# Coefficient tables by direction, the last table block by halves, scan coefficients copied earlier, and early output halves of two blocks kept in SBUF

## The chip, the cores and the metric

The kernel runs on one core of a Trainium2 chip. The metric is the device time of one execution, in microseconds (us). A core has five engines with instruction queues of their own, each in order: TensorE (PE in the profile; PEld is its weight load), VectorE (DVE), ScalarE (ACT), GpSimd (POOL) and SyncE (SP), which here issues DMAs. An instruction starts when its engine has done all that stand ahead of it in the queue and when the semaphores that it waits for are set. A wait therefore also holds whatever stands behind the waiting instruction on that engine.

## The reference

The program is a bidirectional encoder of four layers: an S5 state-space mixer, a gated MLP with a centred convolution, a differential attention layer and a second such MLP, for 512 positions of 1024 channels. The change lies in the S5 mixer alone:

```
u = h.reshape(bsz, seq, 64 groups, 16 channels)
for direction in range(2):
    abar = exp(step * lam)                     # complex, per group and state (64 states)
    bbar = (abar - 1) / lam * b                # complex
    bu   = einsum('blgc,gpc->lbgp', u, bbar)
    s    = associative_scan(abar, bu, reverse=(direction == 1))
    y   += einsum('lbgp,gcp->blgc', s_re, c_re) - einsum('lbgp,gcp->blgc', s_im, c_im)
g = gelu(y);  out = g * sigmoid(g @ glu_w + glu_b)
```

The other three layers are matrix products with norms, a softmax and gates between them.

## The kernel before

One function, `trunk`, holds the whole program. The mixer is worked in chunks of 8 positions: 64 chunks, whose states are chained by a scan of 64 steps, and inside a chunk by a small Toeplitz product.

First come the powers of the coefficients. PRh and PIh hold the powers of abar, FRh and FIh those times the input factor (64 rows of each direction, 8 powers, 64 groups). `cmul` builds powers from powers on VectorE (6 operations); `tok` is the RMS norm's chain of small operations, and `chains` writes several such chains by turns. `ftab` (L369) copies FRh and FIh into a PSUM table F: tag "F", two buffers of one bank each. A table of before holds 16 groups of both directions and takes 8 copies of 64x128; two of the first table's are on VectorE, the others on ScalarE (L385).

Then the block loop (L528) runs over 16 blocks b = (p2, dr): 8 groups of one direction each. In a block VectorE does a product `vmul` (L502, with the first half of F), a product `vmul2` (L509, second half, into PSUM) and their sum (L539). The product of block b+1 is issued ahead of the sum of block b. Every odd block has `kfix` (L516, L518) between, which repairs the kernel block that ScalarE copied in the odd block before. TensorE transposes the sum in two halves (vtp, L547), ScalarE copies each out (vt, L549); between the halves TensorE does `in_mm` of the block before (ips, L476), which ScalarE copies into IZ (L483). After them come the kernel products (kps, L563), copied by ScalarE after odd blocks (kq, L573), and transposed and copied by `kt` (ktp L489; KF, KB L491). At a block's end ScalarE gets table copies: pieces of `ftab` after blocks 3, 4, 7 and 8, and pieces of `tables` (8 copies of PR and PI, L451, which GpSimd needs for the output weights W, and 12 of the scan coefficients sct, L459). GpSimd builds the chunks of W all the while (L431, L433, L436); for five later ones TensorE adds the two parts and ScalarE copies the sum (L441 to L443).

The scan (L661) is a chain on VectorE: two products (L678), two sums (L681, which read IZ) and two sums into the next state (L683) a step. After every 8 steps `states` (L648) writes the states into IZ with 8 copies of 64x256, on ScalarE but for the last four. The list EV says at which step something else is written among these: w is a chunk of W, i is `intra` (L617, the Toeplitz product of output block bk, 16 matmuls), f and b are `out_half` (L633, the state part of rows that are ready early, forward and backward), y is ScalarE's copy of an intra result into SBUF (ys, L657). Since ScalarE works in order, a y that stands ahead of a `states` group delays that group when its own input is late.

After the scan `out_fin` closes the eight output blocks. For 0 to 5 it adds the halves that were missing (L725: 32 matmuls of 32 rows), for 6 and 7, of which only the intra part is in ys, it makes all rows (L713: 32 matmuls of 64 rows), and VectorE adds ys (L732). A gelu (L734), transposes (L746) and casts with a residual split (L750, L751: `chan`) lead to the first matrix product (L778). From there TensorE works nearly without a break to the end of the program.

Of the kernel before, what the change touches and what calls it, by code (L numbers as in the profile page):

```python
# [9 lines left out]
F32 = mybir.dt.float32  # L10
# [27 lines left out]
def trunk(ctx, tc, xs, xt, sp, bx, cx, sv, vec, lamv, biasw, wglu, wup, wdn, wv, wqk, wo, out):  # L38
# [353 lines left out]
    chains(ftab(0))  # L392
    chains(ftab(1))
# [10 lines left out]
    fgen = iter([])  # L404

# [92 lines left out]
    def vmul(b):  # L498
        p2, dr = divmod(b, 2)
        fl = (p2 % 2) * 8  # L500
        vb = vs.tile([128, 8, 8, 16], F32, tag="vb", name="vb", bufs=4)
        V.tensor_tensor(vb, bc(Xb, dr * 64 + p2 * 8), kbc(F[p2 // 2][0][:, dr, :, fl:fl + 8]), op=ALU.mult)  # L502
        return vb

    def vmul2(b):
        p2, dr = divmod(b, 2)
        fl = (p2 % 2) * 8
        vb2 = ps1.tile([128, 8, 8, 16], F32, tag="vb2", name="vb2", bufs=1)
        V.tensor_tensor(vb2, bc(Yb, dr * 64 + p2 * 8), kbc(F[p2 // 2][1][:, dr, :, fl:fl + 8]), op=ALU.mult)  # L509
        return vb2  # L510
# [977 lines left out]
```

## Time and profile before

| | us |
|---|---|
| median of 3 runs | 1249.82 (1247.38 to 1250.08) |
| profiled execution | 1246.88 |
| its span in the trace | 1245.1 |
| busy: PE, DVE, ACT, POOL | 1175.8, 824.9, 581.6, 253.5 |
| block loop 21 to 84: DVE busy of 63.00 | 59.60 |
| scan 92 to 150: DVE busy of 58.00 | 57.82 |
| 200 to 1245: PE busy of 1045.00 | 1027.14 |

The profiled execution is one execution; 1.78 us of it lie around the span. A timeline row has the start, the duration (of all instructions where several are merged, with xcount), the engine, the line, the operation with its tiles (out<-in), and in brackets the idle time just before it and what ended this. The clock column is the clock granted to TensorE as a share of full speed.

### The profile page before, as it was taken

How to read it: one execution, taken by the hardware profiler on the slowest of the kernel's cores; microseconds unless marked ns; L12 is line 12 of the kernel's file. 1: busy time of each engine (PE TensorE's matmuls, PEld its weight loads, DVE VectorE, ACT ScalarE, POOL GpSimd, SP SyncE). 2: the span in 40 equal slices, each digit the busy share in tenths (PEclk: the TensorE clock that was granted, in tenths of full speed). 3: DMA queues.
4: the chain of work that ended last, by engine and by line, in shares of the span. 5: the costliest groups of instructions: out<-in, count | busy, mean ns of one | idle time of the engine just before them, and what ended most of it. 6: DMA issues, size and time to landing. Idle time of an engine off the chain costs nothing.

```text
span 1245.1 us, 16497 instructions
## 1 busy us (share of the span) xinstructions
PE 1175.8 (94%) x6338; PEld 930.0 (75%) x6338; DVE 824.9 (66%) x1650; ACT 581.6 (47%) x1001; POOL 253.5 (20%) x271
## 2 busy tenths in 40 slices
PE   3875899999999999999998999999999999999996
PEld 1663588888878888878876777678888878888786
DVE  7989866676752467754339899976767643566634
ACT  6864655444431244333337777755444422344431
POOL 3899434000000000011033444523000000000011
PEclk8997999999999999999999999999999999999998
DMA  5005322122233222132332323221222233122222
GB/s 219 2 2 136 135 75 102 68 102 84 75 117 115 68 102 101 58 106 77 99 123 82 90 74 87 88 73 67 98 71 99 81 117 125 68 92 78 93 94 68
DMA packets 23391, 112.32 MB, mean 90 GB/s; under 512 B 2704, under 2 KB 5392, under 8 KB 16144
## 3 DMA queue, kind: packets, MB, share of 16 engines
q1 hardware_dynamic: 21472, 108.64, 25.7%
q0 software_dynamic: 1280, 2.10, 0.9%
q8 instruction: 50, 0.82, 0.3%
q10 hardware_dynamic: 560, 0.52, 0.1%
q14 instruction: 29, 0.24, 0.1%
HBM read 102.86 MB, written 2.10 MB: 84 GB/s over the span
## 4 chain that ended last, share of the span: by engine, by line
PE 83%; DVE 14%; ACT 2%; issue 1%; DMA 0%; SPq 0%; DVEq 0%; ACTq 0%
PE ps L779 20%; PE ps L778 20%; PE ps L780 20%; DVE scn L678 2%; PE pj L778 2%; PE pj L780 2%; PE pj L779 2%; DVE St L683 1%; PE vps L1088 1%; DVE qkt L1141 1%; PE vps L1090 1%; PE vps L1089 1%; DVE acc L681 1%; PE po L779 1%; PE po L780 1%; PE po L778 1%
## 5 line engine op out<-in xcount | busy, mean ns | idle before, releaser
L778 PE MATMUL ps<-xhi,hi 128*128 128x512 f32 x672 | 266.9, 397 | 0.0
L779 PE MATMUL ps<-xlo,hi 128*128 128x512 f32 x672 | 265.7, 395 | 0.0
L780 PE MATMUL ps<-xhi,lo 128*128 128x512 f32 x672 | 264.1, 393 | 0.0
L139 ACT ACTIVATE hi<-raw 128x1024 fp32r<-128x1024 f32 (+2 forms) x216 | 184.1, 874 | 113.5 <-PE ps L779 85.8
L141 DVE TENSOR_TENSOR lo<-raw,hi 128x1024 fp32r<-128x1024 f32 (+3 forms) x178 | 188.3, 1077 | 43.5 <-ACT hi L139 41.8
L903 DVE TENSOR_TENSOR tpb<-ps,rb 128x512 f32<-128x512 f32 x88 | 60.8, 693 | 149.7 <-PE ps L780 144.5
L905 ACT ACTIVATE acc<-tpb,vect 128x512 f32<-128x512 f32 x88 | 71.6, 816 | 168.2 <-DVE tpb L903 168.2
L780 PEld LDWEIGHTS ps<-xhi,lo 128*128 128x128 f32 x672 | 126.1, 188 | 31.5
L778 PEld LDWEIGHTS ps<-xhi,hi 128*128 128x128 f32 x672 | 126.1, 188 | 30.6
L779 PEld LDWEIGHTS ps<-xlo,hi 128*128 128x128 f32 x672 | 126.2, 188 | 29.5
L779 PE MATMUL ps<-act,hi 128*128 128x512 f32 (+1 forms) x374 | 144.1, 385 | 0.2
L778 PE MATMUL ps<-act,hi 128*128 128x512 f32 (+1 forms) x374 | 142.8, 382 | 0.0
L780 PE MATMUL ps<-act,lo 128*128 128x512 f32 (+1 forms) x374 | 142.1, 380 | 0.0
L803 POOL COPY ssum<-sqt 128x512 f32<-128x512 f32 x4 | 2.5, 627 | 658.5 <-ACT sqt L800 658.5
L981 DVE TENSOR_TENSOR h<-ps,h 128x512 f32<-128x512 f32 x30 | 20.7, 690 | 107.5 <-PE ps L780 107.5
L141 POOL TENSOR_TENSOR lo<-raw,hi 128x512 fp32r<-128x512 f32 (+1 forms) x38 | 61.0, 1611 | 114.2 <-ACT hi L139 114.1
L778 PEld LDWEIGHTS ps<-act,hi 128*128 128x128 f32 x374 | 70.3, 188 | 15.8
L780 PEld LDWEIGHTS ps<-act,lo 128*128 128x128 f32 x374 | 70.2, 188 | 15.9 <-DVE lo L141 1.4
L779 PEld LDWEIGHTS ps<-act,hi 128*128 128x128 f32 x374 | 70.2, 188 | 15.3 <-DVE act L922 1.1
L911 DVE SCALAR_TENSOR_TENSOR acc<-tpb,vect,acc 128x512 f32<-128x512 f32 x88 | 66.2, 752 | 3.1
L910 DVE SCALAR_TENSOR_TENSOR acc<-tpb,vect,acc 128x512 f32<-128x512 f32 x88 | 65.5, 744 | 0.6 <-ACT acc L905 0.6
L921 ACT ACTIVATE act<-acc 128x512 fp32r<-128x512 f32 x44 | 27.9, 634 | 66.2 <-DVE acc L920 66.2
(260 smaller groups left out, 2035.7 us busy)
## 6 DMA issues: line engine op xcount, KB each, us to landing
raw<-wup SPq DMA_DIRECT2D x44, 1024.0 KB, 4.8
raw<-wdn SPq DMA_DIRECT2D x32, 704.0 KB, 4.0
raw<-wqk SPq DMA_DIRECT2D x16, 512.0 KB, 3.5
raw<-wglu SPq DMA_DIRECT2D x4, 1024.0 KB, 4.9
raw<-wv SPq DMA_DIRECT2D x8, 512.0 KB, 3.5
raw<-wo SPq DMA_DIRECT2D x4, 1024.0 KB, 4.8
bias<-biasw SPq DMA_DIRECT2D x8, 448.0 KB, 4.1
cxt<-cx SPq DMA_DIRECT2D x1, 2064.0 KB, 15.8
```

What stands on the lines that cost most here:

```text
L139: S.activation(hi[:, h0:h1], self.raw[i][:, h0:h1], AF.Copy)
L141: eng.tensor_tensor(lo[:, h0:h1], self.raw[i][:, h0:h1], hi[:, h0:h1].bitcast(F32), op=ALU.subtract)
L678: V.tensor_tensor(prd[dr], cur[:, dr].unsqueeze(1).to_broadcast([128, 2, 2, 32]), cft[dr], op=ALU.mult)
L778: PE.matmul(ps, lhsT=wh, rhs=xh, start=first, stop=False)
L779: PE.matmul(ps, lhsT=wh, rhs=xl, start=False, stop=False)
L780: PE.matmul(ps, lhsT=wl, rhs=xh, start=False, stop=last)
L903: V.tensor_tensor(tb[:, 1:513], ps, state["rb"], op=ALU.mult)
L905: S.activation(acc, tb[:, 1:513], AF.Identity, bias=cb, scale=cw[1])
L910: V.scalar_tensor_tensor(acc, tb[:, 0:512], cw[0], acc, op0=ALU.mult, op1=ALU.add)
L911: V.scalar_tensor_tensor(acc, tb[:, 2:514], cw[2], acc, op0=ALU.mult, op1=ALU.add)
L921: S.activation(hi, a0, AF.Copy)
L981: V.tensor_tensor(h[:, m], ps, h[:, m], op=ALU.add)
```

## The change

1. `ftab(dr, g8)` makes one table for one direction and 32 groups, in 4 copies of 64x256. Two are made at the start, `ftab(0, 0)` and `ftab(1, 0)`. The other two follow at the end of blocks 6 and 7, when the two buffers have been read for the last time. Blocks 0 to 7 read the first two, blocks 8 to 15 the others.
2. The powers 2 and 3 are made ahead of `tok`, those from 4 on by turns with it. The eight PR and PI copies stand after blocks 1 and 2, the sct copies from block 3 on.
3. In block 15 `kfix(6)` comes first, then product and sum by halves of 128x512. The last vtp takes the bank of vb2, and the last two ips have a bank each of tag "F".
4. The copies of the scan's coefficients (`scan_tables`) stand on ScalarE ahead of the last two IZ copies.
5. Output blocks 6 and 7 get intra and both early halves during the scan, late (steps 46 to 53), and are then copied to ys; after the scan `out_fin` makes only their missing halves, as for the others.
6. The last group of states is copied in two parts: 6 of 8 states at step 61, 2 at step 63.

```diff
-    chains(ch_f47(), tok())
+    chains(cmul(FRh[:, 2:4], FIh[:, 2:4], FRh[:, 0:2], FIh[:, 0:2], *pk(2, 2), 2))
+    chains(cmul(FRh[:, 4:8], FIh[:, 4:8], FRh[:, 0:4], FIh[:, 0:4], *pk(4, 4), 4), tok())
...
-    def ftab(g4):
-
-        f = ps1.tile([128, 4, 8, 16], F32, tag="F", name="F", bufs=2)
...
+    def ftab(dr, g8):
+
+        f = F[dr, g8] = ps1.tile([128, 2, 8, 32], F32, tag="F", name="F", bufs=2)
+        for ti, tab in enumerate((FRh, FIh)):
+            src = tab[64 * dr:64 * dr + 64, :, g8 * 32:g8 * 32 + 32]
+            if dr == 0:
+                src = src[:, ::-1]
+            for ri in range(2):
+                dst = f[64 * ri:64 * ri + 64, ti]
+                sg = 1.0 if ri + ti == 0 else -1.0
+                if g8 + dr == 0 and ti == 0:
+                    V.tensor_scalar(dst, src, sg, None, op0=ALU.mult)
+                else:
+                    S.mul(dst, src, sg)
...
-    chains(ftab(0))
-    chains(ftab(1))
+    ftab(0, 0)
+    ftab(1, 0)
...
-            if b == 14:
-                vtt["i"] = ps1.tile([128, 8, 2, 64], F32, tag="vb2", name="ips", bufs=1)
-            ips = vtt["i"][:, 4 * (b - 14):4 * (b - 13)]
+            ips = ps1.tile([128, 4, 2, 64], F32, tag="F", name="ips", bufs=2)
...
-    def vmul2(b):
+    def vmul2(b, vb):
...
+        if b < 15:
+            V.tensor_tensor(vb2, bc(Yb, dr * 64 + p2 * 8), tab, op=ALU.mult)
+            V_next(b)
+            V.tensor_tensor(vb, vb, vb2, op=ALU.add)
+        else:
+            kfix(6)
+
+            for q in range(2):
+                part = slice(4 * q, 4 * q + 4)
+                V.tensor_tensor(vb2[:, part], bc(Yb, dr * 64 + p2 * 8)[:, part], tab[:, part], op=ALU.mult)
+                V.tensor_tensor(vb[:, part], vb[:, part], vb2[:, part], op=ALU.add)
...
+    def V_next(b):
+        nonlocal vnext
+        if b % 2 == 1 and b > 1:
+            kfix(b // 2 - 1)
+        vnext = vmul(b + 1)
...
-                vtp = (ps1.tile([128, 4, 128], F32, tag="F", name="vtp", bufs=2) if last else
+                vtp = (ps1.tile([128, 8, 128], F32, tag="vb2", name="vtp", bufs=1)[:, 0:4] if last else
...
         if b == 15:
+            for _ in tgen:
+                pass
+            scan_tables()
             in_mm(14, vtt.pop(14))
             in_mm(15, vtt.pop(15))
...
-            if b in (3, 7):
-                fgen = ftab(2 + b // 7)
-            for _ in range(4):
-                next(fgen, None)
-            for _ in range((0, 3, 3, 0, 0, 2, 2, 0, 0, 2, 2, 2, 2, 2)[b] if b < 14 else 0):
+            if b in (6, 7):
+                ftab(b - 6, 1)
+            for _ in range((0, 4, 4, 2, 2, 2, 0, 0, 2, 2, 2, 2, 2, 2)[b] if b < 14 else 0):
...
-    EV = ((11, 'w', 8), (12, 'w', 9), (22, 'w', 10), (23, 'i', 7), (23, 'y', 7), (24, 'i', 6), (24, 'y', 6), (25, 'i', 0),
...
+          (38, 'b', 3), (39, 'w', 13), (43, 'w', 14), (44, 'w', 15), (46, 'i', 6), (46, 'f', 6), (47, 'b', 6), (47, 'y', 6),
+          (48, 'i', 4), (48, 'f', 4), (49, 'b', 4), (51, 'i', 7), (52, 'f', 7), (52, 'b', 7), (53, 'y', 7), (54, 'i', 5),
+          (54, 'f', 5), (55, 'b', 5))
...
+        if s == 61:
+            for dr in range(2):
+                states(St, 56, dr, 0, 6)
         if sl == 7:
             for dr in range(2):
-                states(St, s - 7, dr)
+                states(St, s - 7, dr, 6 if s == 63 else 0)
...
     def out_fin(bk):
-        if bk >= NB:
+        if bk in ASIDE:
             yb[bk] = ps2.tile([128, 4, 8, 16], F32, tag="yp", name="yp", bufs=6)
...
-                        PE.matmul(yb[bk][64 * e:64 * e + 64, pl], lhsT=IZ[:, :, dr, e, pr],
-                                  rhs=W[pr // 8][:, dr, (pr % 8) * 2 + e], start=(pl + dr == 0), stop=True,
-                                  skip_group_check=True)
...
+                    PE.matmul(yp[r0:r0 + 32, pl], lhsT=IZ[:, j0:j0 + 32, dr, e, pr],
+                              rhs=W[pr // 8][:, dr, (pr % 8) * 2 + e], start=bk in ASIDE and pl == 0, stop=True,
+                              skip_group_check=True, tile_position=(0, r0))
```

The order changes at three places. The first is on ScalarE and VectorE in blocks 6 and 7. On ScalarE before, from the vt of block 6's first half on (vt_695, ips_697 and vt_720 are of block 7; F_732 is a table that block 12 is the first to read):

```order
L549 COPY vt_636<-vtp_631 128x512
L483 COPY IZ_78<-ips_638 128x64x2x4
L549 COPY vt_661<-vtp_656 128x512
L459 ACTIVATE sct_71<-PRh_212 64x32
L459 ACTIVATE sct_71<-PIh_213 64x32
L549 COPY vt_695<-vtp_690 128x512
L483 COPY IZ_78<-ips_697 128x64x2x4
L549 COPY vt_720<-vtp_715 128x512
L573 COPY kq_730<-kps_663 128x512
L385 ACTIVATE F_732<-tsc_92 64x128 x4
```

ScalarE after, from the same place on (vt_689, ips_691 and vt_714 are of block 7; F_663 is the table of direction 0, F_726 of direction 1):

```order
L562 COPY vt_627<-vtp_622 128x512
L472 COPY IZ_78<-ips_629 128x64x2x4
L562 COPY vt_652<-vtp_647 128x512
L379 ACTIVATE F_663<-tsc_92 64x256 x4
L562 COPY vt_689<-vtp_684 128x512
L472 COPY IZ_78<-ips_691 128x64x2x4
L562 COPY vt_714<-vtp_709 128x512
L589 COPY kq_724<-kps_654 128x512
L379 ACTIVATE F_726<-tsc_92 64x256 x4
```

Two groups of four copies have come in, one ahead of block 7's vt, one behind kq_724. On VectorE before, from the second product of block 7 on (vb_687 and vb_746 are the products of blocks 8 and 9, F_496 was written in blocks 3 and 4):

```order
L509 TENSOR_TENSOR vb2_682<-bxt_93,F_277 128x1024
L516 SCALAR_TENSOR_TENSOR kq_606<-svt_72,kps_545 128x16 x2
L518 TENSOR_TENSOR kq_606<-kq_606,kps_545 128x2x16
L502 TENSOR_TENSOR vb_687<-bxt_93,F_496 128x1024
L539 TENSOR_TENSOR vb_628<-vb_628,vb2_682 128x1024
L509 TENSOR_TENSOR vb2_744<-bxt_93,F_496 128x1024
L502 TENSOR_TENSOR vb_746<-bxt_93,F_496 128x1024
L539 TENSOR_TENSOR vb_687<-vb_687,vb2_744 128x1024
```

VectorE after (vb_681 and vb_740 are the products of blocks 8 and 9, vb_619 the sum of block 7):

```order
L500 TENSOR_TENSOR vb2_676<-bxt_93,F_273 128x1024
L515 SCALAR_TENSOR_TENSOR kq_597<-svt_72,kps_538 128x16 x2
L517 TENSOR_TENSOR kq_597<-kq_597,kps_538 128x2x16
L491 TENSOR_TENSOR vb_681<-bxt_93,F_663 128x1024
L502 TENSOR_TENSOR vb_619<-vb_619,vb2_676 128x1024
L500 TENSOR_TENSOR vb2_738<-bxt_93,F_663 128x1024
L491 TENSOR_TENSOR vb_740<-bxt_93,F_726 128x1024
L502 TENSOR_TENSOR vb_681<-vb_681,vb2_738 128x1024
```

The sequence is the same, but the product of block 8 reads F_663 and stands ahead of the sum of block 7, and that of block 9 reads F_726 and stands ahead of the sum of block 8.

The second place is on ScalarE at the end of the block loop. Before (scn0 and scn1 are the scan's coefficients of the two directions):

```order
L483 COPY IZ_78<-ips_1096 128x64x2x4
L549 COPY vt_1119<-vtp_1114 128x512
L549 COPY vt_1141<-vtp_1136 128x512
L483 COPY IZ_78<-ips_1150 128x64x2x4 x2
L573 COPY kq_1193<-kps_1121 128x512
L491 COPY KF_315<-ktp_1195 128x128
L491 COPY KB_316<-ktp_1195 128x128
L608 COPY scn0_1204<-sct_71 128x64
L609 COPY scn0_1204<-sct_71 128x64
L608 COPY scn1_1207<-sct_71 128x64
L609 COPY scn1_1207<-sct_71 128x64
```

After:

```order
L562 COPY vt_1105<-vtp_1100 128x512
L562 COPY vt_1129<-vtp_1124 128x512
L529 COPY scn0_1138<-sct_71 128x64
L530 COPY scn0_1138<-sct_71 128x64
L529 COPY scn1_1141<-sct_71 128x64
L530 COPY scn1_1141<-sct_71 128x64
L472 COPY IZ_78<-ips_1144 128x64x2x4
L472 COPY IZ_78<-ips_1162 128x64x2x4
L589 COPY kq_1188<-kps_1107 128x512
L480 COPY KF_307<-ktp_1190 128x128
L480 COPY KB_308<-ktp_1190 128x128
```

The four scn copies have moved from behind KF and KB to a place ahead of both IZ copies.

The third is on ScalarE in the last third of the scan, where the groups of eight L648 copies of before, L652 of after, are `states`. Before:

```order
L443 COPY W3_1622<-wa_1626 128x512
L443 COPY W3_1622<-wa_1630 128x512
L443 COPY W3_1622<-wa_1687 128x512
L443 COPY W3_1622<-wa_1691 128x512
L648 COPY IZ_78<-St_1551 64x8x32 x8
L443 COPY W3_1622<-wa_1731 128x512
L443 COPY W3_1622<-wa_1735 128x512
L648 COPY IZ_78<-St_1695 64x8x32 x8
L648 COPY IZ_78<-St_1792 64x8x32 x8
L648 COPY IZ_78<-St_1874 64x8x32 x4
```

After:

```order
L434 COPY W3_1589<-wa_1654 128x512
L434 COPY W3_1589<-wa_1658 128x512
L652 COPY IZ_78<-St_1518 64x8x32 x8
L434 COPY W3_1589<-wa_1698 128x512
L434 COPY W3_1589<-wa_1702 128x512
L661 COPY ys_1367<-yp_1728 128x512
L652 COPY IZ_78<-St_1662 64x8x32 x8
L661 COPY ys_1367<-yp_1818 128x512
L652 COPY IZ_78<-St_1760 64x8x32 x8
L652 COPY IZ_78<-St_1893 64x6x32 x4
L652 COPY IZ_78<-St_1893 64x2x32 x4
```

Two ys copies have come in, each ahead of a group of states, and the last group is in two parts.

## Rows read from the trace of the kernel before

**Rows 1.** Windows by stage: length, busy time of each engine, TensorE clock, DMA share, GB/s

```profile
21.00:84.00 63.00, 48.56 (x832) 37.24 (x832) 59.60 (x70) 45.75 (x113) 56.40 (x47) 0.90 0.01 2
...
200.00:1245.00 1045.00, 1027.14 (x4611) 821.10 (x4609) 658.61 (x1042) 457.25 (x714) 126.04 (x183) 1.00 0.27 90
```

**Rows 2.** Timeline of the start: start, duration, engine, line, operation, [idle before]

```profile
21.35 4.25 ACT L385 ACTIVATE F<-tsc 64x128 f32<-64x128 f32 x14 [1.10 <-DVE F L383]
...
23.19 1.22 DVE L502 TENSOR_TENSOR vb<-bxt,F 128x1024 f32<-128x1024 f32 x1 [1.87 <-ACT F L385]
...
44.48 0.37 DVE L516 SCALAR_TENSOR_TENSOR kq<-svt,kps 128x16 f32<-128x16 f32 x2 [0.41 <-ACT kq L573]
```

**Rows 3.** Timeline of VectorE in blocks 6 to 9

```profile
49.64 1.22 DVE L539 TENSOR_TENSOR vb<-vb,vb 128x1024 f32<-128x1024 f32 x1
...
52.53 1.21 DVE L502 TENSOR_TENSOR vb<-bxt,F 128x1024 f32<-128x1024 f32 x1
...
53.66 1.21 DVE L539 TENSOR_TENSOR vb<-vb,vb 128x1024 f32<-128x1024 f32 x1
...
56.05 1.21 DVE L502 TENSOR_TENSOR vb<-bxt,F 128x1024 f32<-128x1024 f32 x1
```

**Rows 4.** Timeline: ScalarE table copies, and GpSimd waiting for one

```profile
37.59 0.63 ACT L451 ACTIVATE PR<-PRh 64x512 f32<-64x512 f32 x1
...
52.81 2.02 POOL L431 TENSOR_TENSOR w<-cxt,PI 128x1024 f32<-128x1024 f32 x1 [5.39 <-ACT PI L451]
...
58.62 1.20 ACT L385 ACTIVATE F<-tsc 64x128 f32<-64x128 f32 x4
```

**Rows 5.** Timeline of TensorE: after two idle stretches, and at the other clock

```profile
27.96 1.12 PE L547 MATMUL vtp<-ident,vb 128*128 128x128 f32 x4 [12.34 <-DVE vb L539]
...
32.86 1.73 PE L476 MATMUL ips<-u,vt 128*64 128x64 f32 x32
...
53.67 0.66 PE L547 MATMUL vtp<-ident,vb 128*128 128x128 f32 x4 [0.67 <-ACT vt L549]
...
151.72 0.43 PE L725 MATMUL yp<-W,IZ 128*32 128x128 f32 x2 [2.84 <-ACT IZ L648]
```

**Rows 6.** A window on TensorE alone: length, busy, granted clock, DMA share, GB/s

```profile
151.70:158.00 6.30, 5.87 (x129) 0.73 0.56 226
```

**Rows 7.** Timeline of the end of the block loop and the first scan step

```profile
86.49 0.58 ACT L483 COPY IZ<-ips 128x512 f32<-128x512 f32 x1 [0.93 <-PE ips L476]
...
87.12 1.20 PE L476 MATMUL ips<-u,vt 128*64 128x64 f32 x32 [0.68 <-ACT IZ L483]
...
90.48 0.69 DVE L678 TENSOR_TENSOR scn<-St,scn 128x128 f32<-128x128 f32 x2 [4.29 <-ACT scn L609]
...
91.34 0.34 DVE L683 TENSOR_TENSOR St<-scn,acc 128x64 f32<-128x64 f32 x2
```

**Rows 8.** Timeline of the scan: ScalarE's copies, TensorE's output blocks

```profile
123.13 0.58 ACT L657 COPY ys<-yp 128x512 f32<-128x512 f32 x1
...
123.72 3.35 ACT L648 COPY IZ<-St 64x256 f32<-64x256 f32 x8
...
143.67 1.09 PE L617 MATMUL yp<-TT,u 128*64 128x128 f32 x16 [1.18 <-ACT W L443]
...
144.13 8.37 ACT L648 COPY IZ<-St 64x256 f32<-64x256 f32 x20
...
147.27 1.61 PE L633 MATMUL yp<-W,IZ 128*32 128x128 f32 x32
```

**Rows 9.** Timeline after the scan

```profile
152.56 5.40 PE L725 MATMUL yp<-W,IZ 128*32 128x128 f32 x126 [0.41 <-ACT IZ L648]
...
158.92 2.00 PE L725 MATMUL yp<-W,IZ 128*32 128x128 f32 x64
...
161.87 3.90 PE L713 MATMUL yp<-W,IZ 128*64 128x128 f32 x64
...
165.82 0.69 DVE L732 TENSOR_TENSOR ys<-yp,ys 128x512 f32<-128x512 f32 x1 [0.40 <-PE yp L713]
```

More of the change, by code (lines that the diff above doesn't have):

```diff
@@ L520, in trunk, with scan_tables @@
     WOPS = {5: 6, 6: 6, 9: 12}
-    EV = ((11, 'w', 8), (12, 'w', 9), (22, 'w', 10), (23, 'i', 7), (23, 'y', 7), (24, 'i', 6), (24, 'y', 6), (25, 'i', 0),
[3 rows of a table removed]
+    acc = [s5c.tile([128, 2, 32], F32, name=f"acc{i}") for i in range(2)]
+    cft, prd = [], []
+    def scan_tables():
+        for dr in range(2):
+            scn = psc.tile([128, 4, 2, 2, 32], F32, tag="st"[dr], name=f"scn{dr}", bufs=1)
+            cft.append(scn[:, 0])
+            prd.append(scn[:, 1])
+            S.copy(cft[dr][:, 0], sct[:, 32 * dr:32 * dr + 32].unsqueeze(1).to_broadcast([128, 2, 32]))
+            S.copy(cft[dr][:, 1], sct[:, 64 + 64 * dr:128 + 64 * dr].rearrange("p (i r) -> p i r", i=2)[:, ::-1])
+    EV = ((11, 'w', 8), (12, 'w', 9), (22, 'w', 10), (23, 'i', 0), (24, 'i', 1), (25, 'i', 2), (26, 'i', 3), (30, 'w', 11),
[4 rows of a table added]
     PC, C0 = (8, 10, 12, 13, 14), 8
@@ L599, in trunk @@
     yb = {}
-    acc = [s5c.tile([128, 2, 32], F32, name=f"acc{i}") for i in range(2)]
-    cft, prd = [], []
-    for dr in range(2):
-        scn = psc.tile([128, 4, 2, 2, 32], F32, tag="st"[dr], name=f"scn{dr}", bufs=1)
-        cft.append(scn[:, 0])
-        prd.append(scn[:, 1])
-        S.copy(cft[dr][:, 0], sct[:, 32 * dr:32 * dr + 32].unsqueeze(1).to_broadcast([128, 2, 32]))
-        S.copy(cft[dr][:, 1], sct[:, 64 + 64 * dr:128 + 64 * dr].rearrange("p (i r) -> p i r", i=2)[:, ::-1])
     def intra(bk):
@@ L656, in trunk @@
     for at_s, kind, bk in EV:
-        f = {"w": wchunk, "i": lambda bk=bk: intra(bk), "y": lambda bk=bk: S.copy(ys[:, bk - NB], yb.pop(bk)), "f": lambda bk=bk: out_half(bk, 0, 0),
+        f = {"w": wchunk, "i": lambda bk=bk: intra(bk), "y": lambda bk=bk: S.copy(ys[:, bk - 6], yb.pop(bk)), "f": lambda bk=bk: out_half(bk, 0, 0),
              "b": lambda bk=bk: out_half(bk, 1, 1)}[kind]
@@ L683, in trunk @@
                 V.tensor_tensor(nx[:, dr], prd[dr][:, 1, ::-1], acc[dr], op=ALU.add)
+        if s == 61:
+            for dr in range(2):
+                states(St, 56, dr, 0, 6)
         if sl == 7:
             for dr in range(2):
-                states(St, s - 7, dr)
+                states(St, s - 7, dr, 6 if s == 63 else 0)
             St = Sn
@@ L754, in trunk @@
     ws.split(1, eng=G)
-    for bk in range(8):
-        out_fin(bk)
-        if bk in (3, 5, 7):
-            chan(bk // 2 - 1)
+    for blk in range(4):
+        out_fin(2 * blk)
+        out_fin(2 * blk + 1)
+        if blk > 0:
+            chan(blk - 1)
     chan(3)
```

76 lines of the change are left out of this document (21 added, 55 removed), and 4 rows, old and new, of the table EV.

## The prediction

> **What bounds the kernel now.** I read the windows by stage first, then the timeline of each stage that the change touches. From 200 us on TensorE works 1027.14 of 1045.00 us at full clock [rows 1]; nothing of the change is there, so whatever the mixer gains or loses ahead of its first matrix product arrives at the end unchanged. In the block loop VectorE is busy 59.60 of 63.00 us [rows 1], and the reader is to see in its timeline that products and sums follow one another without idle time in brackets [rows 3]. A microsecond in which VectorE waits there is lost, and one that ScalarE or TensorE loses is not, as long as VectorE doesn't wait for it. At the loop's end VectorE idles 4.29 us for ScalarE's copies of the scan's coefficients [rows 7]. Through the scan VectorE is again the chain; its end is set by ScalarE's copies of states, of which the last 20 run without a break from 144.13 to 152.50 [rows 8]. Then TensorE and VectorE close the output blocks [rows 9].
>
> **The start.** Before, the first product waits for the sixth of 14 copies on ScalarE, at 23.19 [rows 2]. A copy of 64x128 takes 0.30 us in a row (1.20 for four), one of 64x512 0.63 [rows 4]; between them, 64x256 comes to 0.41, and the state copies of that size take 0.42 (3.35 for eight) [rows 8]. After, two such copies do, and powers 2 and 3 are done sooner, so that I place ScalarE's start at 21.1 (estimate) and the product at 21.94: 1.25 us earlier. But VectorE waited 0.41 us at 44.48 for ScalarE's kq in block 3 [rows 2], and ahead of that kq ScalarE now has eight PR and PI copies instead of six, 2 x 0.62 more [rows 4]. That is the same 1.25. I take zero; the bounds are -1.2 (another engine's slack swallows the copies) and 0.
>
> **The waits for the new tables.** This is the largest term. The product of block 8 reads the table that ScalarE copies behind the second vt of block 6, and that vt needs the sum of block 6. In the trace the sum of block 7 ends at 54.87 [rows 3] and the table copies that stood at the end of that block began at 58.62 [rows 4], 3.75 later; a kq copy of 128x512, 0.58 by the ys copy of that size [rows 8], was between, which block 6 doesn't have, so some 3.16 there. The sum of block 6 ends at 50.86 [rows 3]; copies from 54.02, four times 0.41, ready at 55.66. The product of block 8 starts at about 55.70 instead of 52.53 [rows 3]: +3.17.
>
> Behind it on VectorE stands the sum of block 7. It therefore ends at 55.70 + 1.13 + 1.21 = 58.04 instead of 54.87. The second table stands behind block 7's kq: it starts 3.75 later, at 61.79, and is ready at 63.43. The product of block 9 starts at 63.50 instead of 56.05 [rows 3]: **+7.45**, the first wait included. The second wait is so long because the first delays the sum on which the second table's place in the queue hangs. Could a table be ready sooner? A product that needed only the first two of four copies would save 2 x 0.82 = 1.6 in all; I keep that as the lower end, 5.8. If ScalarE is behind, each table comes later by what it is behind; I give +1 for that.
>
> The Trainium skill says (ScalarE: Activation LUTs, "What ACT_TABLE_LOAD costs") that an ACTIVATE with immediate scale takes 186 ns and 0.833 ns an element, and that neighbours overlap by some 93 ns. An estimate from that page is 0.31 us apart for 64x256 and tables ready some 0.35 us sooner each, so a sum lower by 0.7. The trace disagrees on the overlap: four copies of 64x128 took 1.20 us [rows 4], where the page would have about 0.9.
>
> **The clock.** During the first wait TensorE has nothing to do from about 54.0 (end of block 6's products) to 58.1, 4.1 us. After 12.34 us of idleness the transposes took 1.12 us and the ips 1.73, against 0.66 and 1.20 otherwise [rows 5, 7]; after 2.84 us the window had a granted clock of 0.73 [rows 5, 6], a mean of the two levels, 1.2 and 2.4 GHz. So I take the lower level for block 7, which is on the path to the second table: two groups of transposes +0.46 each, ips +0.53, the kernel products about +0.45 (by the ratio of the transposes), together +1.9, and the product of block 9 starts at 65.4. The bounds are 0 and 1.9. TensorE idles a second time before block 8's transposes; what it loses then is not waited for at once, since sums and transposes have buffers between them: 0, bounds 0 and +1.2.
>
> The Trainium skill states (TensorE: Matmul & The Clock Gate, "What's actually happening") that half rate is the default and that activity releases it, which speaks for this term; by that rule the sum keeps its 1.9, and without it the second rival below holds.
>
> **The end of the loop.** From block 10 on VectorE has its old sequence, so the lag of 9.35 passes to block 15. Its halves bring nothing that I can see: the first transposes of block 15 wait for ScalarE as before, not for the sum. What comes is in the rows of the last two ips. Before, the second ips waits 0.68 us for the first IZ copy and starts at 87.12; then come its IZ copy, kq, KF, KB, and four scn copies, of which VectorE's first scan product waits, and the first new state stands at 91.34 [rows 7]. After, the four scn copies, each smaller than the 0.30 us copies of [rows 4], lie beside the first ips of 1.20, the second ips follows at 86.45 without that wait, the IZ copies end at 87.07 and 88.28 (0.58 each [rows 7]), and the first state stands at 88.47: **-2.87**. That is from the old clock; bounds -3.2 and -1.5 (a scn copy that comes late).
>
> **The scan.** GpSimd's first chunk no longer waits 5.39 us for a PI table [rows 4], and two ys copies (0.58 each) no longer stand ahead of the states of step 31 [rows 8]; so TensorE reaches the late sets some 3.5 us earlier than the 143.67 of before, at about 140.0 on the old clock. It then has a set of 1.09 + 1.61 = 2.7 us [rows 8] four times. The third set, block 7, ends at 148.25, and its ys copy at 148.9. Only behind that come the eight copies of step 55 (3.35), four of 64x192 (0.36 each, by the slope above) and four of 64x64 (0.26): 148.9 + 3.35 + 1.44 + 1.04 = 154.7, where the last copy ended at 152.50 [rows 8]: **+2.2**. So the split of the last group saves less than the ys copy ahead of it costs. Bounds: -0.6 if TensorE is so early that the scan alone sets the end, and +4.5 if the late sets begin only 1.2 us earlier. A second idle stretch of TensorE opens ahead of the first halves (intra 0 to 3 are done early, the halves wait for step 31), some 3.5 us; at the lower level two sets of halves cost twice: +0.8, bounds 0 and +1.6.
>
> **After the scan.** Blocks 6 and 7 go from 64 matmuls in 3.90 us to 64 of the L725 kind in 2.00 [rows 9], -1.9 on TensorE. But the last ys sum, at 165.82, had waited only 0.40 us for TensorE [rows 9]; until then VectorE had other work, so it can come only that much earlier. I take **-0.4**, bounds 0 and -1.9. The clock may stay up here if TensorE idles less before this stage: 126 matmuls took 5.40 us, at the rate of the next row 3.94 [rows 9], so up to -1.46, in the lower bound alone.
>
> **The sum.** 7.45 + 1.9 - 2.87 + 2.2 + 0.8 - 0.4 = +9.1. The profiled execution took 1246.88 (span 1245.1 and 1.78 around it), so 1256.0 by its own time. It is faster than the three timed runs, 1247.38 to 1250.08; the middle of the four is 1248.5, and I forecast **1257.6**.
>
> **The rivals.**
> First, TensorE's clock stays up in both idle stretches. For it: they are no longer than 4.1 us and what fell to 0.73 after 2.84 us is one place. Then 9.1 - 2.7 = +6.4, 1254.9.
> Second, the waits are short: the start's 1.2 counts, the products need half a table, the clock stays. 5.8 - 1.2 - 2.87 + 2.2 - 0.4 = +3.5, 1252.0. Against it: each is a choice against a row.
> Third, more is lost: the end of the loop gives only 1.5, or the late sets begin late (+4.5 rather than 2.2). +10.4 to +12.7, about 1260.
> Fourth, on the other side: the tables are ready when they are read. The mechanism is ScalarE's place in blocks 6 and 7; if its table copies ran as soon as the buffers are free, the waits would go. Then -2.87 - 0.4 - 1.46 - 0.6 = -5.3, 1243.2. It decides where both waits together stay under 2.8 us (up to 5.3 the time is no longer than before). Against it: each table stands behind a vt or kq of its own block on an engine that works in order, and the 3.75 us from a sum to that place are in the rows.
> Fifth, the change does not do what it says: the earlier scan start is there but kq and KF of the last block, now behind the IZ copies, hold GpSimd and TensorE. That would leave +9 to +10, inside the forecast's own range.
>
> **How the numbers follow.** Forecast with the fifth 0.42, first 0.26, second 0.11, third 0.14, fourth 0.07. About 0.2%, 2.5 us, is what a measurement of this kernel can tell from no change. Faster by more: the fourth, 0.07. Within: the low part of the second, 0.08. Slower: 0.85. The range 1251.5 to 1261.0 holds all but the fourth, the low end of the second and the top of the third.
>
> **What would show it.** VectorE's products of blocks 8 and 9 should have idle time in brackets, released by ScalarE's F, of about 3.2 and 4.3 to 6.2 us, with vtp of block 7 at 1.1 us; the first state should stand some 6.5 us later than before, at about 98; ScalarE should be busy to the end of step 63 with a ys copy about 3.3 us ahead of its last states; the last ys sum should be some 9 us later. No idle time at block 8 would make the prediction wrong in its main term; vtp of 0.66 in block 7 in the clock's.

## The result, and the profile after

The changed kernel is slower: 1256.45 us in the median of six executions (1255.59 to 1257.10) against 1249.31 (1247.38 to 1250.08), a ratio of 1.0059, 95% interval 1.0046 to 1.0072. That is +7.1 us; the forecast was 1257.6, in a range of 1251.5 to 1261.0. The profiled execution took 1256.62 us (span 1254.8) beside 1246.88 (span 1245.1) of before. Of the 9.7 us between the spans 8.05 lie ahead of the first matrix product. The rest is in the attention stage, where the profile of before had the full clock and that of after had 0.97 in two windows; before's profiled execution was also faster than each of its six timed ones. Of the experiments below, one execution of e9 fell into a slow state (1472.88 us at a mean granted clock of 0.75); it is in no range and no ratio, and only in the median of e9, which is 1251.59 without it.

The stations, from the two traces:

| | before | after | difference | forecast |
|---|---|---|---|---|
| first product | 23.19 | 21.98 | -1.2 | -1.25 |
| product of block 8 | 52.53 | 56.26 | +3.7 | +3.2 |
| product of block 9 | 56.05 | 66.19 | +10.1 | +9.35 |
| first new state | 91.34 | 98.33 | +7.0 | +6.5 |
| end of the last state copy | 152.50 | 162.65 | +10.15 | +9.5 |
| first matrix product (L778) | 168.07 | 176.12 | +8.05 | +9.1 |

The timeline of the changed kernel's VectorE shows the wait for the kq of block 3 and the two waits for the tables (the rows of before: [rows 2, 3]; a product of before, L502, is now L491):

```profile
45.04 0.37 DVE L515 SCALAR_TENSOR_TENSOR kq<-svt,kps 128x16 f32<-128x16 f32 x2 [1.57 <-ACT kq L589]
...
56.26 1.22 DVE L491 TENSOR_TENSOR vb<-bxt,F 128x1024 f32<-128x1024 f32 x1 [3.09 <-ACT F L379]
57.39 1.21 DVE L502 TENSOR_TENSOR vb<-vb,vb 128x1024 f32<-128x1024 f32 x1
...
66.19 1.22 DVE L491 TENSOR_TENSOR vb<-bxt,F 128x1024 f32<-128x1024 f32 x1 [6.32 <-ACT F L379]
```

Both idle stretches end with ScalarE's F. On ScalarE and TensorE, in the same stretch, the tables stand where the order put them, and the work of block 7 between is slow:

```profile
54.60 1.62 ACT L379 ACTIVATE F<-tsc 64x256 f32<-64x256 f32 x4
...
58.75 1.09 PE L560 MATMUL vtp<-ident,vb 128*128 128x128 f32 x4 [4.28 <-DVE vb L502]
...
59.77 2.03 PE L465 MATMUL ips<-u,vt 128*64 128x64 f32 x32
...
61.73 1.12 PE L560 MATMUL vtp<-ident,vb 128*128 128x128 f32 x4
...
62.78 1.08 PE L579 MATMUL kps<-vb,cxt 128*32 128x128 f32 x16
...
64.54 1.62 ACT L379 ACTIVATE F<-tsc 64x256 f32<-64x256 f32 x4
```

After 4.28 us without work TensorE ran at the lower level, as after the idle stretches of [rows 5]; the window says 0.57 (columns as in [rows 1]: length, busy time and count of PE, PEld, DVE, ACT and POOL, granted clock, DMA share, GB/s):

```profile
58.70:66.00 7.30, 6.15 (x60) 4.59 (x60) 1.17 (x1) 3.71 (x8) 7.14 (x4) 0.57 0.00 0
```

The end of the loop and the first state, where before had 4.29 us of idle time for the scn copies [rows 7]:

```profile
96.63 0.59 ACT L472 COPY IZ<-ips 128x512 f32<-128x512 f32 x1
...
97.57 0.59 ACT L472 COPY IZ<-ips 128x512 f32<-128x512 f32 x1 [0.34 <-PE ips L465]
...
98.18 0.23 DVE L685 TENSOR_TENSOR acc<-scn,IZ 128x64 f32<-128x64 f32 x1 [0.70 <-ACT IZ L472]
98.33 0.34 DVE L687 TENSOR_TENSOR St<-scn,acc 128x64 f32<-128x64 f32 x2
```

VectorE now waits for the IZ copies themselves, and from the product of block 9 to the first state it takes 32.14 us instead of 35.29. In the scan the early halves run after an idle stretch in part at the lower level (granted clock 0.72 from 129 to 135), and the ys copies stand ahead of the states (beside [rows 8]). The halves before:

```profile
127.13 2.11 PE L633 MATMUL yp<-W,IZ 128*32 128x128 f32 x46 [0.41 <-ACT IZ L648]
```

The halves, the ys copies and the states after:

```profile
128.36 0.43 PE L637 MATMUL yp<-W,IZ 128*32 128x128 f32 x2 [3.92 <-ACT IZ L652]
...
130.88 3.10 PE L637 MATMUL yp<-W,IZ 128*32 128x128 f32 x46 [0.20 <-ACT IZ L652]
...
151.16 0.59 ACT L661 COPY ys<-yp 128x512 f32<-128x512 f32 x1 [2.30 <-PE yp L637]
151.77 3.32 ACT L652 COPY IZ<-St 64x256 f32<-64x256 f32 x8
...
156.24 0.59 ACT L661 COPY ys<-yp 128x512 f32<-128x512 f32 x1 [1.15 <-PE yp L637]
156.85 5.80 ACT L652 COPY IZ<-St 64x256 f32<-64x256 f32 x16
```

The 46 matmuls took 3.10 us, 1.0 us more than before. Each ys copy waited for TensorE (2.30 and 1.15) with the states of steps 47 and 55 ready behind it. After the scan (beside [rows 9]):

```profile
162.18 4.26 PE L724 MATMUL yp<-W,IZ 128*32 128x128 f32 x128 [2.67 <-ACT IZ L652]
...
170.35 2.00 PE L724 MATMUL yp<-W,IZ 128*32 128x128 f32 x64
...
173.28 1.28 DVE L731 TENSOR_TENSOR ys<-yp,ys 128x512 f32<-128x512 f32 x2
```

Blocks 6 and 7 take 2.00 us instead of 3.90 [rows 9]. That brings 0.4 us at the last ys sum, which no longer waits for TensorE (0.40 before [rows 9]). More is from the first four blocks, which ran at full clock here (1.00, where [rows 6] has 0.73): 4.26 us where before needed 0.43 and 5.40. They end 3.79 us after the last state copy instead of 5.46, 1.7 sooner.

### The profile page after: what moved, and what is told of

Same layout as the page of the kernel before. It is cut to its first block, busy times and chain, and to the rows that moved or that the text cites. A ratio compares the mean times of both kernels' runs of the same rounds, so it can differ in the third digit from the quotient of the medians.

```text
span 1254.8 us, 16628 instructions
## 1 busy us (share of the span) xinstructions
PE 1184.2 (94%) x6402; PEld 935.3 (75%) x6402; DVE 826.2 (66%) x1656; ACT 580.0 (46%) x989; POOL 253.2 (20%) x271
## 4 chain that ended last, share of the span: by engine, by line
PE 83%; DVE 13%; ACT 2%; issue 1%; DMA 0%; DVEq 0%; ACTq 0%
PE ps L778 20%; PE ps L780 20%; PE ps L779 20%; PE pj L778 2%; PE pj L780 2%; PE pj L779 2%; DVE scn L682 2%; PE po L779 1%; PE po L778 1%; PE po L780 1%; PE vps L1088 1%; PE vps L1089 1%; PE vps L1090 1%; DVE qkt L1141 1%; DVE St L687 1%; PE ptp L1242 1%
## 5 line engine op out<-in xcount | busy, mean ns | idle before, releaser
L778 PE MATMUL ps<-xhi,hi 128*128 128x512 f32 x672 | 266.5, 397 | 0.0
L778 PEld LDWEIGHTS ps<-xhi,hi 128*128 128x128 f32 x672 | 126.2, 188 | 30.1
L778 PE MATMUL ps<-act,hi 128*128 128x512 f32 (+1 forms) x374 | 142.8, 382 | 0.0
L778 PEld LDWEIGHTS ps<-act,hi 128*128 128x128 f32 x374 | 70.3, 188 | 14.9
```

What stands on the lines that cost most here:

```text
L778: PE.matmul(ps, lhsT=wh, rhs=xh, start=first, stop=False)
```

## The experiments

The start of a profile moves by up to 2 us between executions (the first product stood between 21.98 and 24.20), so the stages are counted from the first product: to the first new state (loop), from there to the end of the last state copy (scan), and to the first matrix product (outputs). Differences of two stations from the profiles, in us; the last columns are the medians of the timed executions and the ratio to the kernel before, whose medians beside the three groups (e1 to e4, e5 to e9, e10 to e12) were 1248.63, 1249.56 and 1248.95. The ratio is not exactly the quotient of the two medians (for e9 that would be 1.0017).

| kernel | loop | scan | outputs | sum | median | ratio, 95% interval |
|---|---|---|---|---|---|---|
| before | 68.15 | 61.16 | 15.57 | 144.88 | 1249.31 | |
| changed | 76.35 | 64.32 | 13.47 | 154.14 | 1256.45 | 1.0059 (1.0046 to 1.0072) |
| e1_old_tables | 65.75 | 68.23 | 13.43 | 147.41 | 1252.12 | 1.0026 (1.0016 to 1.0036) |
| e2_tables_alone | 78.37 | 59.92 | 15.97 | 154.26 | 1258.01 | 1.0068 (1.0052 to 1.0085) |
| e3_sum_first | 70.88 | 63.76 | 15.09 | 149.73 | 1251.34 | 1.0025 (1.0009 to 1.0040) |
| e4_no_idle | 74.74 | 63.79 | 15.11 | 153.64 | 1254.74 | 1.0041 (1.0025 to 1.0057) |
| e5_old_outputs | 75.46 | 59.94 | 15.86 | 151.26 | 1255.89 | 1.0050 (1.0034 to 1.0067) |
| e7_late_ys | 75.44 | 61.49 | 13.44 | 150.37 | 1252.54 | 1.0030 (1.0019 to 1.0040) |
| e8_scn_behind | 77.71 | 63.81 | 16.09 | 157.61 | 1260.32 | 1.0090 (1.0075 to 1.0105) |
| e9_tables_early_w | 66.79 | 63.93 | 15.82 | 146.54 | 1251.64 | 1.0008 (0.9993 to 1.0024) |
| e10_tables_late_ys | 67.65 | 60.52 | 13.44 | 141.61 | 1245.55 | 0.9964 (0.9953 to 0.9974) |
| e11_tables_old_out | 67.47 | 59.94 | 15.71 | 143.12 | 1246.27 | 0.9968 (0.9956 to 0.9980) |
| e12_filled | 67.30 | 61.59 | 15.41 | 144.30 | 1246.92 | 0.9977 (0.9967 to 0.9987) |

**The tables undone, and the tables alone.** e1 takes part 1 out of the changed kernel and puts the PR, PI and sct copies back at their old places; e2 puts the same two things alone into the kernel before. Of e1's edit, without the lines of `ftab` itself and of its readers:

```diff
...
-            if b in (6, 7):
-                ftab(b - 6, 1)
-            for _ in range((0, 4, 4, 2, 2, 2, 0, 0, 2, 2, 2, 2, 2, 2)[b] if b < 14 else 0):
+            if b in (3, 7):
+                fgen = ftab(2 + b // 7)
+            for _ in range(4):
+                next(fgen, None)
+            for _ in range((0, 3, 3, 0, 0, 2, 2, 0, 0, 2, 2, 2, 2, 2)[b] if b < 14 else 0):
```

> The changed kernel with part 1 alone undone: tables of 16 groups and both directions, copied in blocks 3, 4, 7 and 8, and the PR, PI and sct copies where they stood before. Theory (the two waits for the new tables cost what the trace shows, 10.1 us at the product of block 9, and the rest of the change gains): no idle time at the products of blocks 8 and 9, first new state near 88.5 us instead of 98.3, and a time of 1256.4 - 10.1 = 1246.3, some 3 us under the kernel before. Rival (most of the wait is swallowed by later slack, the loss sits in the scan's end): 1251 to 1254. Rival (the scan's later copies are only hidden because the loop is late, so the gain is lost again at the scan's end): about 1249, same as before.

> The kernel before with part 1 alone: tables by direction, copied at the start and in blocks 6 and 7, and the PR, PI and sct copies at their new places; nothing else of the change. Theory: the product of block 9 waits as in the changed kernel, 10 us later than before, and nothing behind gives it back: 1249.3 + 10 = 1259.3. Rival (the loss needs the other parts as well): 1253 to 1256.

e2 came as expected, 1.3 under its forecast: its loop is 10.2 us longer than before's, with idle times of 3.09 and 6.18 at the two products. e1 lost the waits (loop 65.75, 10.6 less) and did not come out ahead: 1252.12, +3.5 instead of -3. The time lies in the first rival's range, but the second rival, that the gain is lost again at the scan's end, comes nearest in mechanism, and the loss was larger than it said. The scan stage of e1 took 68.2 us, 7.1 more than before's. The rows of e1 say why: GpSimd's second chunk of W waits for a PI table, and at the start of the scan TensorE waits for GpSimd.

```profile
54.52 2.02 POOL L427 TENSOR_TENSOR w<-cxt,PI 128x1024 f32<-128x1024 f32 x1 [5.39 <-ACT PI L447]
...
104.23 2.08 PE L437 MATMUL wa<-W,ident 128*128 128x512 f32 x2 [11.80 <-POOL W L429]
```

**One instruction moved.** e3 leaves the tables where the change put them and lets the sum of block 7 go ahead of the product of block 8.

```diff
+            if b == 7:
+                V.tensor_tensor(vb, vb, vb2, op=ALU.add)
             V_next(b)
-            V.tensor_tensor(vb, vb, vb2, op=ALU.add)
+            if b != 7:
+                V.tensor_tensor(vb, vb, vb2, op=ALU.add)
```

> The changed kernel with one instruction moved: the product of block 8 stands behind the sum of block 7 on VectorE, not ahead of it. Theory (the first wait holds the sum on which the second table's place on ScalarE hangs, so the two waits add up): the sum of block 7 ends near 54.4 us, the second table is ready near 60.5, the product of block 9 starts there instead of at 66.2, and the time is 1256.4 - 5.7 = 1250.7. Rival (the second table is late by ScalarE's own queue): the product of block 9 moves by less than 2 us, 1255 or more.

Measured 1251.34, 5.1 less than the changed kernel. That median is not a sharp number: seven of the twelve executions lie between 1249.4 and 1251.5 (mean granted clock 0.980 to 0.981), five between 1254.5 and 1255.0 (0.977). The rows of e3's VectorE around the two products:

```profile
53.36 1.22 DVE L502 TENSOR_TENSOR vb<-vb,vb 128x1024 f32<-128x1024 f32 x1
56.91 1.22 DVE L491 TENSOR_TENSOR vb<-bxt,F 128x1024 f32<-128x1024 f32 x1 [1.83 <-ACT F L379]
58.05 1.22 DVE L500 TENSOR_TENSOR vb<-bxt,F 128x1024 f32<-128x1024 f32 x1
61.01 1.22 DVE L491 TENSOR_TENSOR vb<-bxt,F 128x1024 f32<-128x1024 f32 x1 [1.74 <-ACT F L379]
```

The waits are 1.83 and 1.74 instead of 3.09 and 6.32, with the same tables at the same places on ScalarE. Counted from the first product, that of block 9 stands 5.8 us earlier, as expected. With the sum out of the first wait TensorE had work earlier, too, and the transposes and ips of block 7 ran fast:

```profile
55.28 0.66 PE L563 MATMUL vtp<-ident,vb 128*128 128x128 f32 x4 [0.16 <-ACT vt L565]
55.87 1.20 PE L465 MATMUL ips<-u,vt 128*64 128x64 f32 x32
```

So the second wait was long because the first held the sum behind it, in two ways: the sum came late, and TensorE, left idle by that, did the work of block 7 at the lower clock. The next experiment tells the two apart.

**The clock.** e4 repeats the kernel products of block 6, so that TensorE is busy while VectorE waits.

```diff
-            for q in range(2):
+            for q in [0, 1] * (7 if b == 6 else 1):
```

> The changed kernel with the kernel products of block 6 done seven times instead of once (the same numbers into the same place), 3.9 us more on TensorE just where it idled 4.3 us ahead of block 7's transposes. Theory (the idle stretch lowers the clock, and the slower transposes, ips and kernel products of block 7 lengthen the second wait by some 2.4 us): transposes of block 7 at 0.66 and ips at 1.20 us, the product of block 9 near 63.8 instead of 66.2, time 1254.0. Rival (ScalarE sets the second table, not TensorE): the clock stays up, the product of block 9 stays within 0.5 us of 66.2, time 1256.

The timeline of e4's TensorE in blocks 6 and 7, and the window of block 7 (columns as above):

```profile
54.38 3.26 PE L579 MATMUL kps<-vb,cxt 128*32 128x128 f32 x112
59.31 0.63 PE L560 MATMUL vtp<-ident,vb 128*128 128x128 f32 x4 [1.67 <-DVE vb L502]
59.87 1.20 PE L465 MATMUL ips<-u,vt 128*64 128x64 f32 x32
```

```profile
58.80:66.00 7.20, 3.50 (x60) 2.69 (x60) 3.04 (x4) 4.22 (x10) 7.04 (x4) 0.99 0.00 0
```

The clock stayed up and the transposes and ips are fast. From the product of block 8 to that of block 9 it is 7.74 us (56.82 to 64.56) instead of 9.93: 2.2 us were the clock's. In e3 it is 4.10, so that the late sum itself makes the other 3.6. The clock's share is not the same in every execution: e7 and e8 below leave block 7 as it is, and there it is 8.99 and 9.02, because the second transposes of block 7 were fast again (0.66). The median of e4 fell by 1.7, to 1254.74 where 1254.0 was expected.

**The outputs and the ys copies.** e5 undoes parts 5 and 6. e7 keeps them and moves the two ys copies behind the states of their step, and the sets of block 5 with the second:

```diff
-(47, 'y', 6),
+(48, 'y', 6),
...
-(53, 'y', 7), (54, 'i', 5), (54, 'f', 5), (55, 'b', 5))
+(56, 'y', 7), (56, 'i', 5), (56, 'f', 5), (57, 'b', 5))
```

> The changed kernel with parts 5 and 6 undone: blocks 6 and 7 get only their intra part, at steps 23 and 24, out_fin makes all their rows after the scan, and the last states are copied in one group at step 63. In the trace of the changed kernel the last state copy ends 64.3 us after the first new state, in the kernel with the tables alone 59.9. Theory (the late ys copies hold ScalarE's state copies): 59.9 to 61 here, so the last copy 3.3 to 4.4 us earlier, of which the longer out_fin takes back about 2.1: 1256.4 - 1.2 to - 2.3 = 1254.1 to 1255.2. Rival (the scan's end hangs on the chunks of W, whatever the outputs do): the last copy stays where it is and the time rises by 2, to 1258.5.

> The changed kernel with the two ys copies moved on ScalarE: block 6's behind the states of step 47 (written at step 48), block 7's behind those of step 55 (written at step 56, and the sets of block 5 with it). Theory (the ys copies, waiting for TensorE, hold the state copies behind them): the states of step 47 start behind the last chunk copy near 149 instead of 151.8, the last state copy ends near 159.5 instead of 162.65, and TensorE starts out_fin there: 1256.4 - 2.7 = 1253.7. Rival (the state copies are late for another reason, such as ScalarE's copies of W): under 1 us, 1256.

e5's edit is the list EV, `out_fin` and `states` as they were:

```diff
-    ASIDE = (6, 7)
+    NB = 6
...
-        if s == 61:
-            for dr in range(2):
-                states(St, 56, dr, 0, 6)
...
```

Both shorten the scan stage, to 59.94 and 61.49. e5 pays it back in the outputs (15.86), and its median, 1255.89, is within 0.6 of the changed kernel, above the 1254.1 to 1255.2 expected; the profiled execution, 1253.07, is the fastest of its four. e7 keeps the short outputs too: 1252.54, 3.9 less, where 2.7 were expected. In its profile 2.8 us of that are in the scan stage, as expected; 0.9 is in the loop, which the edit does not touch, where the clock rose sooner in block 7. ScalarE's and TensorE's timeline at the end of e7's scan:

```profile
151.96 0.62 ACT L661 COPY ys<-yp 128x512 f32<-128x512 f32 x1
152.61 3.34 ACT L652 COPY IZ<-St 64x256 f32<-64x256 f32 x8
...
157.63 1.61 PE L637 MATMUL yp<-W,IZ 128*32 128x128 f32 x32
159.07 3.78 PE L724 MATMUL yp<-W,IZ 128*32 128x128 f32 x128
```

No ys copy waits, and TensorE goes from the last halves into the first output blocks without a break, 128 matmuls in 3.78 us.

**The scan's coefficients.** e8 moves the call of `scan_tables` behind the loop.

```diff
-            scan_tables()
             in_mm(14, vtt.pop(14))
...
+    scan_tables()
     yb = {}
```

> The changed kernel with part 4 undone: the four copies of the scan's coefficients stand behind kq, KF and KB on ScalarE again; the separate banks of the last two ips stay. Theory: the first new state stands 2.3 us later, near 100.6 instead of 98.3; the states of step 31, for which TensorE waits 3.9 us in the changed kernel, are later by as much, and so is the end: 1258.7. Rival (the scan's end hangs on GpSimd's chunks and TensorE, not on the scan's start): the first new state moves by 2.3, the end by less than 1: 1257.

The first scan product of e8 in VectorE's timeline waits again (first row; the second is of the outputs):

```profile
99.01 0.69 DVE L682 TENSOR_TENSOR scn<-St,scn 128x128 f32<-128x128 f32 x2 [3.34 <-ACT scn L530]
...
178.15 1.97 PE L745 MATMUL tr<-ident,Y 128*128 128x128 f32 x8 [2.09 <-ACT Y L733]
```

From the product of block 9 to the first state it is 34.36 us, 2.2 more, as expected, and from there on 1.7 of it are left at the last state copy (98.17 instead of 96.46 from that product). The median is 1260.32, 3.9 over the changed kernel; the 2.6 us by which the outputs are longer are the clock again (128 matmuls in 5.92 us instead of 4.26, the last eight transposes in 1.97 instead of 1.09), which neither theory had.

**The chunks of W.** e9 is e1 with the PR and PI copies, and the sct copies behind them, where the change put them.

```diff
-            for _ in range((0, 3, 3, 0, 0, 2, 2, 0, 0, 2, 2, 2, 2, 2)[b] if b < 14 else 0):
+            for _ in range((0, 4, 4, 2, 2, 2, 0, 0, 2, 2, 2, 2, 2, 2)[b] if b < 14 else 0):
```

> The kernel e1_old_tables (the changed kernel with the tables of before) with the eight PR and PI copies at the changed kernel's places, after blocks 1 and 2. In e1 the loop lost its waits, but the scan part took 68.2 us from the first new state to the last state copy instead of 64.3, and GpSimd idled 5.39 us for a PI table. Theory (with the loop short again, the end of the scan hangs on GpSimd's chunks of W, which start when the PI copies are there): GpSimd's second chunk 5.4 us earlier, the first sum of chunks on TensorE earlier by as much, the last state copy some 3.3 us earlier: 1252.1 - 3.3 = 1248.8. Rival (the chunks are not what TensorE waits for; the late outputs of part 5 are): no change, 1252.

The same two rows in e9's timeline:

```profile
47.60 2.03 POOL L427 TENSOR_TENSOR w<-cxt,PI 128x1024 f32<-128x1024 f32 x1
...
97.40 2.08 PE L437 MATMUL wa<-W,ident 128*128 128x512 f32 x2 [4.59 <-POOL W L429]
```

Counted from the first product, the second chunk stood 6.3 us earlier, the first sum of chunks 6.2, and the scan stage became 4.3 us shorter, more than expected. With the 2.8 of the ys copies (e7) that makes 7.1, the whole of what e1's scan stage had over before's. The median was 1251.64 all the same, 0.5 less instead of 3.3: 1.0 us went in the loop (VectorE waited 1.57 us for the kq of block 3, which stands behind the copies) and 2.4 in the outputs, at the lower clock. Nine executions ranged from 1247.3 to 1252.9, so the mechanism is shown by the trace and its worth is not by the times.

**The costs added up.** e10 has the old tables, the moved ys copies, and of the eight PR and PI copies six where they were before, two after block 3. e11 has the outputs of before instead of the moved copies. e12 is e10 with 16 transposes of the identity ahead of out_fin. The first diff is the place of the copies in all three, against the changed kernel.

```diff
-            for _ in range((0, 4, 4, 2, 2, 2, 0, 0, 2, 2, 2, 2, 2, 2)[b] if b < 14 else 0):
+            for _ in range((0, 3, 3, 2, 2, 2, 0, 0, 0, 2, 2, 2, 2, 2)[b] if b < 14 else 0):
```

```diff
...
+    filler(4)
     for blk in range(4):
         out_fin(2 * blk)
```

> The changed kernel with the tables of before (as e1), the ys copies behind the states (as e7), and two of the eight PR and PI copies after block 3 instead of after blocks 1 and 2 (so that no copy more than before stands ahead of block 3's kq). Theory (the costs add up, each from its own trace, counted from the first product: first new state at 65.8 us as in e1, last state copy 61.5 later as in e7, first matrix product 13.4 to 13.5 later where TensorE has no idle stretch before out_fin): 140.8 us from the first product to the first matrix product against 144.9 before, so 4.1 us under the kernel before, about 1245.2. Rival (GpSimd's chunks, which the shorter loop leaves behind, set the scan's end): 64 instead of 61.5, 1247.7 to 1250.

> As e10_tables_late_ys, with the outputs of before (parts 5 and 6 undone as in e5) in place of the moved ys copies; what is left of the change is the order of the powers, block 15 by halves, the separate ips banks, the earlier scn copies and the earlier PR and PI copies. Theory: 65.8 + 59.9 + 15.7 = 141.4 us from the first product to the first matrix product, 3.5 us under the kernel before, about 1246, and 0.6 over e10. Rival (the scan's earlier start is worth nothing, its end hangs on the chunks of W): 1249, same as before.

> As e10_tables_late_ys, with 16 transposes of the identity, some 2.6 us of TensorE's time with no reader, ahead of out_fin. Theory (a short idle stretch there sometimes brings the lower clock; the kernels with the late ys copies had 2.67 us of it, and out_fin's first 128 matmuls took 4.26 us in two profiles and 5.92 in three): the first 128 matmuls at 3.8 to 4.3 us in every run, and no run of the upper group, so a median equal to e10's or up to 1.5 lower. Rival (the extra transposes end behind the last state copy and delay out_fin): 0.5 to 1.5 more than e10.

e10 came to 1245.55, 0.3 over its forecast, the lowest median; e11 to 1246.27, where 1246 was expected, and their ranges overlap. In e10's profile two misses partly cancel, the loop 1.9 us over its forecast and the scan 1.0 under. e10 and e11 both beat the kernel before with intervals clear of one. Their loops are 1.7 to 1.9 longer than e1's: VectorE waits 2.0 us in block 7 for the kq of block 5, which stands behind the extra copies of blocks 3 and 4. What e10 has left at the end of the scan:

```profile
149.50 1.44 ACT L659 COPY IZ<-St 64x192 f32<-64x192 f32 x4
149.53 1.09 PE L628 MATMUL yp<-TT,u 128*64 128x128 f32 x16 [0.69 <-ACT ys L668]
150.55 1.61 PE L644 MATMUL yp<-W,IZ 128*32 128x128 f32 x32
151.16 1.02 ACT L659 COPY IZ<-St 64x64 f32<-64x64 f32 x4 [0.22 <-DVE St L694]
151.99 3.98 PE L731 MATMUL yp<-W,IZ 128*32 128x128 f32 x128
```

Now the scan itself ends last (0.22 behind VectorE's state), and TensorE has no gap. e12's rival was right. The transposes began when the last halves ended and held out_fin by 1.9 us:

```profile
151.75 1.97 PE L673 MATMUL fill<-ident 128*128 128x128 f32 x16
153.65 3.74 PE L740 MATMUL yp<-W,IZ 128*32 128x128 f32 x128
```

So the median is 1.4 higher though the 128 matmuls took 3.74. As e10's profile had no gap to fill there, e12 does not test what a gap does; and its profile has 1.1 us more in the scan, where 62 matmuls of the first halves took 5.37 us against e10's 4.09.

## Why the prediction was right, point by point

The main term was right in place and size. Both products wait for ScalarE's F, 3.09 and 6.32 us, and the sum between carries the first wait into the second (e3). The forecast was +7.45 at full clock and +1.9 for the clock; the trace has +10.14. The 0.8 between are two sizes: kq in block 3 came 0.56 later than before, where I had taken the start's gain and the extra copies to be equal, with bounds of -1.2 and 0, so that the start cost something rather than nothing (VectorE waited 1.2 us longer for that kq, as the copies forecast, but also 0.83 instead of 0.23 us for the kq of block 1, which I had not looked at); and the ips of block 7 took 2.03 us, not 1.73. The copies took 1.62 for four, as I had worked out (1.64).

The clock's term was right: e4 gives 2.2 for the 1.9 of block 7, in this profile; e7 and e8 had 1.3. The first rival, without it, falls by these rows. By the time alone it would not: 1256.45 lies 1.15 under the forecast and 1.55 over that rival. It is the first rival and not the second, as the prediction has it beside the clock's term, that holds without it.

The end of the loop gave 3.15 for 2.87, and e8 puts 2.2 of it on the scn copies. That the halves of block 15 bring nothing was not tried by itself; nor were the order of the powers (part 2) and the split of the last states (part 6).

The scan's part was right in sum: +3.16 for 2.2 + 0.8. e7 shows that the ys copies make 2.8 of it; the halves ahead of them ran in part at the lower clock as forecast, but what that alone costs at the scan's end was not tried.

The term that was mis-sized is the last, "I take -0.4, bounds 0 and -1.9 ... up to -1.46, in the lower bound alone" for the outputs: the profile shows -2.1. The -0.4 itself came, and came again where the clock was low ahead of out_fin as it was before: 15.09 and 15.11 us in e3 and e4 against 15.57. The other 1.7 is the clock, which I had at nothing in the sum, and it stayed up in this profile. It is not a fixed gain. The same edit gave outputs of 13.4 to 13.5 us in the profiles of the changed kernel and of e1, and 15.1 to 16.1 in those of e3, e4, e8 and e9.

So the sum came near in part by luck: the +0.8 at block 9 and the -1.7 at the outputs have opposite signs, and the second is a clock level that another execution need not have. The traces give +8.05 and the medians +7.1 for the +9.1 of the sum.

The fourth rival was right on its mechanism only in part. Without the waits the time would have been 1243.2 by its sum; e1 measured 1252.12. Its working took the scan's end as bound by the scan alone (-0.6), but with the loop 10 us shorter GpSimd's chunks, which keep their own pace, become the bound (e1, e9). That chain was in the trace of before, as the PI wait in [rows 4], and I had used it only as a gain of the change. The third and the second rival fall with the sizes above, and so does the fifth: kq, KF and KB behind the IZ copies hold nobody that matters, since the scan's start stays 3.15 earlier, and GpSimd's next chunk, which waits 8.48 us and starts at 101.00, is released by VectorE's state (St, L687).

## What to carry to other kernels

Where a table has two buffers, its next copy can't start before the last read of the old one, and on an engine that works in order it also stands behind everything queued since; count that from the sum that releases the queue, and ask which instruction is held behind the first wait, because it may release the second. When a stage is shortened, look for the engine that runs through it at its own pace (here GpSimd's chunks): it takes the gain unless it is started earlier too. A copy that waits for a late producer belongs behind the copies that are ready, which was worth 2.8 us of the scan stage here for moving five list entries.

## What the runs showed that I had not expected

An idle stretch of the same length had both outcomes: 2.67 to 2.69 us ahead of the first output blocks were followed by 128 matmuls in 4.25 or 4.26 us (changed kernel, e1) and in 5.92 or 5.93 us (e3, e4, e8, e9). In the profiles of e1 (first row) and e3:

```profile
157.65 4.25 PE L731 MATMUL yp<-W,IZ 128*32 128x128 f32 x128 [2.67 <-ACT IZ L659]
...
156.79 5.92 PE L727 MATMUL yp<-W,IZ 128*32 128x128 f32 x128 [2.67 <-ACT IZ L655]
```

Why is open. It makes some 2 us of a single execution's time a matter of chance, and in the attention stage the two profiled executions differ in the same way, in two windows of 0.97 against 1.00, which cost 1.7 us. The timed executions vary with their mean granted clock, too: the 27 of the kernel before beside the last group go from 1247.2 (0.982) to 1253.1 (0.977). So a difference of 2 us between two single profiles of this kernel proves nothing by itself; the experiments above rest on rows of the stage that was changed. Where TensorE had no gap at all (e7, e10), the 128 took 3.78 and 3.98.
